# Where three small sums are made in a hybrid encoder layer: pooling additions on VectorE, x split by token groups, norms by a product with ones

## The chip, the cores and the metric

The kernel runs on one core of a Trainium2 chip. The metric is the device time of one execution in microseconds (us). Five engines work side by side, each through its own queue in order: TensorE (PE, with its weight load PEld), VectorE (DVE), ScalarE (ACT), GpSimd (POOL) and SyncE (SP), which issues most DMAs. The median of three runs before the change is 1566.14 us (1560.39 to 1567.87).

## The reference

One layer of a streaming encoder is computed for 1024 prompt tokens and 64 sample tokens, 1088 together, with a model width of 1024, all in fp32:

```python
h = rms_norm(x, norm_mix_g)
q, fl, iv, og, ca, cg, pu = split(h @ w_in)       # 4 x 512, 3 x 256 wide
a_out = hgrn2(q, fl, iv) normed, * silu(og)       # 4 heads, per-token recurrence
b_out = silu(layer_norm(depthwise_conv31(ca * sigmoid(cg))))
c_out = ((window_sum(pu, w) / count - pu) @ pool_w) * pool_scale   # w = 2, 4, 8, 16
x = x + concat(a_out, b_out, c_out) @ w_out
x = x + cross_attention(rms_norm(x, norm_x_g), mem_k, mem_v)       # 256 memory tokens
x = x + square(relu(rms_norm(x, norm_ffn_g) @ w_up)) @ w_down
y = rms_norm(x, final_g)

def rms_norm(x, g):
    return x * rsqrt(mean(x * x, axis=-1) + 1e-6) * g
```

Memory keys and values of the prompt are made from `mem_prompt` by a norm and two projections, and are outputs too, as are the new recurrent state and the last rows of the convolution and the pooling.

## The kernel before, in words

Activations lie transposed: 8 tiles of 128 features by 1088 tokens. Each fp32 operand is split into a high part (`hi`, `wh`) and a low part (`lo`, `wl`), and a product is three matmuls (`mm3`, all recorded under L210). ACT writes the high part, DVE subtracts it to get the low one. A weight block of 128 output features (1024 columns) passes through `prep`: ACT writes `wh`, DVE `wl`, and SP loads the next block. Three split blocks can be held at a time. `dense` multiplies one block with all of x in three groups of 364, 364 and 360 tokens; with `across` the three groups advance together through the 8 input tiles, otherwise group by group. PSUM banks come in two sets of four, `psd` for dense products and `psm` for the rest.

`memory` makes keys, then values (the V loop, 8 blocks, 12 products of 512 columns each). Beside the V loop x is normalised: for each of its 8 tiles DVE multiplies all 1088 tokens by the row `rb` of reciprocal roots, ACT writes `hi` scaled by the gain, DVE writes `lo`. During `memory` and the attention the order on each engine is the order in the program (`inorder`); elsewhere a list scheduler sets it from its own estimate of times.

`mixers` projects h: first the convolution's two pairs (a sigmoid gate `csig` and a product `glu`, for two halves), then per head a gate f and a query q, with the pooling inputs `pu` after head 1. The work of the heads (`head`: 7 levels of a decay tree with PE products and DVE multiplies of `fn` and `q`, then states), of the convolution (`conv`) and of the pooling (`pool`) is fed in pieces between dense products. `pool` makes window sums by doubling: two additions for the half with windows 2 and 4, four for the half with 8 and 16, and one copy each of 64 partitions, all on POOL; then DVE forms the difference to `pu` and PE multiplies it with `poolw`.

A norm of squares summed over tiles in `acc` takes two passes on PE. `rstd_cols` multiplies blocks of 128 tokens of `acc`, as the stationary operand, with one column of ones, so the sums of 128 tokens lie on 128 partitions; ACT takes the root of a few columns, DVE the reciprocal. `bcast_cols` then spreads each column over a row by a product with the identity, and ACT copies the row from PSUM to SBUF. An fp32 product shows as two records. This happens for the attention (1088 tokens), for each half of 544 tokens before the MLP (`rstd_half`, into the tile `masks`), and for three final groups of 416, 416 and 256 tokens.

The MLP (`up`) multiplies by a scheme with 7 products for 8. Its jobs need sums of weight halves (`sw`, `wr`) and split operands (`df`, `th`, `tl`); its outputs are scaled by `masks` on DVE. In the last part each final group adds its tiles to `xr` on DVE, ACT squares them, DVE adds the squares to `facc`, and POOL multiplies `xr` by the row of reciprocal roots before it is stored; the last group is finished by POOL and DVE together.

## Time and profile before

| | |
|---|---|
| median of the runs | 1566.14 us (1560.39 to 1567.87) |
| profiled execution, its time | 1564.72 us |
| profiled execution, its span | 1562.9 us |
| mean granted clock of PE | 0.993 |
| DMA | 150.58 MB, 27.3% of 16 engines' span on the main queue |

The page has the busy time of each engine in the span, and a chain of work followed back from the last instruction. Windows give the same busy times for a stretch, with the granted clock of PE (1.00 is full). In rows of single instructions the first number is the start, the second the length, and the square bracket holds the idle time of the engine before it, with what ended it. In grouped rows the first number behind the bar is the total busy time, the second the mean in ns of one. A length includes some overlap with the next instruction, so the spacing of starts is a little less.

### The profile page before, as it was taken

The numbers are of one execution on the slowest core, as the hardware profiler recorded it, in microseconds if no ns is written. First come the engines' busy times: TensorE is split into PE (matmuls) and PEld (weight loads), VectorE is DVE, ScalarE is ACT, GpSimd is POOL, SyncE is SP. The second block draws the span as 40 slices with busy tenths as digits, with TensorE's granted clock in tenths as the row PEclk, the third lists the DMA queues.
The fourth block names the chain that finished last, engine by engine and source line by source line (L and its number), as shares of the span: only waits on it lengthen the run. The fifth ranks groups of instructions, "written<-read, shape, count | busy, mean of one in ns | idle before, by whom it ended". The sixth has DMA issues, their size and how long they took to land.

```text
span 1562.9 us, 24283 instructions
## 1 busy us (share of the span) xinstructions
PE 1532.2 (98%) x10204; PEld 1486.5 (95%) x10204; DVE 902.6 (58%) x1329; ACT 587.5 (38%) x1072; POOL 123.2 (8%) x101
## 2 busy tenths in 40 slices
PE   8999999999999999999998999999999999999997
PEld 7799898999999999989998999999999999999997
DVE  7638988375654433684579545555585444434434
ACT  7422213556372222463555344444463111111133
POOL 0100001200000000000001222222100000000005
PEclk9999999999999999999999999999999999999999
DMA  9421011010013311223532233232286223211003
GB/s 347 137 83 55 15 41 32 18 41 18 31 66 145 127 55 55 68 78 113 184 113 97 98 112 112 98 112 85 98 320 241 99 100 109 94 59 53 29 1 115
DMA packets 54941, 150.58 MB, mean 96 GB/s; under 512 B 6704, under 2 KB 14384, under 8 KB 54832
## 3 DMA queue, kind: packets, MB, share of 16 engines
q1 hardware_dynamic: 51952, 148.37, 27.3%
q8 instruction: 80, 1.31, 0.3%
q10 hardware_dynamic: 2880, 0.66, 0.2%
q14 instruction: 29, 0.24, 0.0%
HBM read 115.11 MB, written 33.91 MB: 95 GB/s over the span
## 4 chain that ended last, share of the span: by engine, by line
PE 85%; issue 6%; DVE 4%; ACT 2%; POOL 1%; DMA 1%; SPq 0%; POOLq 0%; ACTq 0%; DVEq 0%
PE psd L210 66%; PE psm L210 13%; PE psm L560 3%; POOL xr L137 1%; DVE wl L138 1%; ACT hi L126 1%; PE psm L638 1%; DVE x L138 1%; PE psm L612 0%; PE psm L640 0%; PE psm L542 0%; DMA t<-tt 0%; PE psd L881 0%; DMA wr<-wk 0%; ACT L126 0%
## 5 line engine op out<-in xcount | busy, mean ns | idle before, releaser
L210 PE MATMUL psd<-hi,wl 128*128 128x364 f32 (+3 forms) x1536 | 507.0, 330 | 0.3 <-DVE wl L138 0.3
L210 PE MATMUL psd<-lo,wh 128*128 128x364 f32 (+3 forms) x1536 | 506.2, 330 | 0.9 <-DVE lo L141 0.9
L210 PE MATMUL psd<-hi,wh 128*128 128x364 f32 (+3 forms) x1536 | 505.4, 330 | 1.5 <-ACT hi L126 0.8
L126 ACT ACTIVATE wh<-wr 128x1024 fp32r<-128x1024 f32 (+1 forms) x178 | 160.5, 905 | 483.9 <-PE psd L210 342.8
L210 PEld LDWEIGHTS psd<-hi,wh 128*128 128x128 f32 x1536 | 288.8, 188 | 3.5 <-ACT hi L126 1.5
L210 PEld LDWEIGHTS psd<-lo,wh 128*128 128x128 f32 x1536 | 289.1, 188 | 2.2 <-DVE lo L141 1.5
L210 PEld LDWEIGHTS psd<-hi,wl 128*128 128x128 f32 x1536 | 289.0, 188 | 1.4 <-DVE wl L138 0.6
L138 DVE TENSOR_TENSOR wl<-wr,wh 128x1024 fp32r<-128x1024 f32 (+1 forms) x178 | 185.8, 1049 | 125.3 <-ACT wh L126 125.0
L138 DVE TENSOR_TENSOR xr<-psd,xr 128x364 f32<-128x364 f32 (+3 forms) x192 | 102.0, 533 | 177.4 <-PE psd L210 177.2
L210 PE MATMUL psd<-th,wh 128*128 128x272 f32 x448 | 130.6, 292 | 1.9 <-ACT wh L126 0.8
L210 PE MATMUL psm<-th,wh 128*128 128x272 f32 x448 | 130.4, 292 | 1.9 <-ACT wh L126 1.1
L210 PE MATMUL psd<-th,wl 128*128 128x272 f32 x448 | 129.7, 291 | 2.4 <-DVE wl L138 2.3
L210 PE MATMUL psd<-tl,wh 128*128 128x272 f32 x448 | 129.2, 289 | 0.0
L210 PE MATMUL psm<-th,wl 128*128 128x272 f32 x448 | 129.2, 290 | 0.0
L210 PE MATMUL psm<-tl,wh 128*128 128x272 f32 x448 | 129.1, 289 | 0.0
L210 PEld LDWEIGHTS psm<-th,wh 128*128 128x128 f32 x448 | 84.5, 189 | 3.4 <-ACT wh L126 1.5
L210 PEld LDWEIGHTS psd<-th,wh 128*128 128x128 f32 x448 | 84.6, 189 | 3.1 <-DVE t L138 1.1
L210 PEld LDWEIGHTS psd<-th,wl 128*128 128x128 f32 x448 | 84.4, 189 | 3.2 <-DVE wl L138 3.2
L210 PEld LDWEIGHTS psd<-tl,wh 128*128 128x128 f32 x448 | 84.7, 189 | 0.0
L210 PEld LDWEIGHTS psm<-tl,wh 128*128 128x128 f32 x448 | 84.7, 189 | 0.0
L210 PEld LDWEIGHTS psm<-th,wl 128*128 128x128 f32 x448 | 84.4, 189 | 0.0
L141 DVE SCALAR_TENSOR_TENSOR cacc<-glu,vecs,cacc 128x1118 f32<-128x1118 f32 x60 | 80.6, 1379 | 0.5
(249 smaller groups left out, 2375.0 us busy)
## 6 DMA issues: line engine op xcount, KB each, us to landing
wr<-w_up SPq DMA_DIRECT2D x38, 512.0 KB, 3.9
tt<-t SPq DMA_DIRECT2D x32, 544.0 KB, 3.1
t<-tt SPq DMA_DIRECT2D x32, 544.0 KB, 5.0
wr<-w_down SPq DMA_DIRECT2D x32, 512.0 KB, 3.3
wr<-w_in SPq DMA_DIRECT2D x18, 512.0 KB, 3.2
x<-res SPq DMA_DIRECT2D x16, 544.0 KB, 2.8
wr<-xo SPq DMA_DIRECT2D x16, 512.0 KB, 3.4
x<-xT SPq DMA_DIRECT2D x8, 544.0 KB, 8.3
```

The source lines that it names most:

```text
L126: return self.inorder("act", lambda: self.nc.scalar.activation(out, in_, f, **kw))
L137: return self.inorder("pool", lambda: eng.tensor_tensor(out, a, b, op))
L138: return self.inorder("dve", lambda: self.nc.vector.tensor_tensor(out, a, b, op))
L141: return self.inorder("dve", lambda: self.nc.vector.scalar_tensor_tensor(out, in0, s, in1, op0, op1))
L210: return self.inorder("pe", lambda: self.nc.tensor.matmul(*args, **kw))
L560: mm(pv[:m, c], k[:, c * P:c * P + m], qc[:, :, 1, :], start=True, stop=True)
L638: mm(ps[:w, c * P:c * P + P], sc[:w, s:s + w], vt[:w, s:s + P], start=True, stop=first)
```

## The change

Three edits. The six additions of `pool` move from POOL to DVE; the two copies of 64 partitions stay on POOL. x is normalised and split in 24 pieces, all tiles of the first token group, then of the second, then of the third, with the low part of a piece issued after the multiply of the next one; two pieces go into each round of the V loop from its third on, the other 12 behind it. The first three projections (`csig`, `glu`, `csig`) are multiplied group by group with three weights held, the fourth as before. And `rstd_rows` gets the sums of a segment by one product of a 128x128 matrix of ones with `acc`, which leaves them on all partitions; ACT takes the root of the whole row and DVE its reciprocal. It is used for the attention, both halves before the MLP and the first two final groups; the norms of the memory, of x and of the last group keep the column form.

```diff
+    def rstd_rows(self, sqs, dim, segs=SEGS, rb=None, tag="m"):
+        if rb is None:
+            rb = self.slot(n="rb")
+        for t0, m in segs:
+            ps = self.bank(tag)
+            for i, sq in enumerate(sqs):
+                self.mm(ps[:, :m], self.ones, sq[:, t0:t0 + m], start=i == 0, stop=i == len(sqs) - 1)
+            r = rb[:, t0:t0 + m]
+            self.act(r, ps[:, :m], AF.Sqrt, scale=1.0 / dim, bias=self.eps)
+            self.inorder("dve", lambda: self.nc.vector.reciprocal(r, r))
         return rb
...
             elif k == X_ROWS:
                 rx = self.bcast_rows(r_x, "d")
                 self.act(self.warm, self.eps, AF.Sigmoid)
+                pieces = [(j, g) for g in GROUPS for j in range(KT)]
+                steps = self.normed(hs, pieces, rx)
             if k >= X_ROWS:
-                self.scale_x(k - X_ROWS, rx)
-                hs.append(self.normed(k - X_ROWS))
+                for _ in range(2):
+                    next(steps)
...
-    def normed(self, k):
-        x = self.xraw[k][:, :T]
-        return self.hl(x, self.vec("mix_g", k))
+    def normed(self, hs, pieces, rb):
+        late = None
+        for k, (t0, m) in pieces:
+            if t0 == 0:
+                hs.append((self.slot(F32R, n="hi"), self.slot(F32R, n="lo")))
+            x, (hi, lo) = self.xraw[k][:, t0:t0 + m], (y[:, t0:t0 + m] for y in hs[k])
+            gain = self.vec("mix_g", k)
+            self.tt(x, x, rb[:, t0:t0 + m], MUL)
+            self.act(hi, x, AF.Copy, scale=gain)
+            if late:
+                self.stt(*late)
+            late = (lo, x, gain, hi.bitcast(F32), MUL, SUB)
+            yield
+        self.stt(*late)
...
-            self.dense(self.weights(), xs, ks, plain(sig, AF.Sigmoid), across=first)
+        while len(self.wq) < 3:
+            self.prep()
+        ws, self.wq = self.wq, []
...
+        for g in GROUPS:
+            for w, ev in zip(ws, evs):
+                self.dense(w, xs, ks, ev, groups=[g])
+        for _ in range(2):
+            self.prep()
+        self.dense(self.weights(), xs, ks, evs[3])
...
-        self.tt(s[:, 1:n], pu[:, 1:n], pu[:, 0:n - 1], ADD, gp)
+        self.tt(s[:, 1:n], pu[:, 1:n], pu[:, 0:n - 1], ADD)
...
     def rstd_half(self, c):
-        r = self.rstd_cols([self.accs[c]], CT, D, "m")
-        yield
-        for tts, c0 in ((CT[:4], 0), (CT[4:], 4)):
-            ps = self.bank("m")
-            t0, m = tts[0][0], sum(x[1] for x in tts)
-            self.bcast_cols(ps, r, tts, t0, c0)
-            self.act(self.rb[:, c, t0:t0 + m], ps[:, :m], AF.Copy)
-        yield
+        for seg in ((0, 512), (512, H - 512)):
+            self.rstd_rows([self.accs[c]], D, [seg], self.rb[:, c])
+            yield
...
+            else:
+                acc = self.rstd_rows([acc], D, [(0, m)])
```

How the order moves, at three places. On DVE in the V loop (x are the tiles of x, `wl` the low parts of the next weights), two rounds before:

```order
L138 TENSOR_TENSOR wl_564<-wr_474,wh_563 128x1024
L138 TENSOR_TENSOR x_126<-x_126,rb_541 128x1088
L141 SCALAR_TENSOR_TENSOR lo_583<-x_126,vecs,hi_582 128x1088
L138 TENSOR_TENSOR wl_587<-wr_493,wh_586 128x1024
L138 TENSOR_TENSOR x_148<-x_148,rb_541 128x1088
L141 SCALAR_TENSOR_TENSOR lo_606<-x_148,vecs,hi_605 128x1088
```

and now:

```order
L138 TENSOR_TENSOR wl_568<-wr_474,wh_567 128x1024
L138 TENSOR_TENSOR x_148<-x_148,rb_541 128x364
L141 SCALAR_TENSOR_TENSOR lo_563<-x_126,vecs,hi_562 128x364
L138 TENSOR_TENSOR x_165<-x_165,rb_541 128x364
L141 SCALAR_TENSOR_TENSOR lo_586<-x_148,vecs,hi_585 128x364
L138 TENSOR_TENSOR wl_596<-wr_493,wh_595 128x1024
L138 TENSOR_TENSOR x_203<-x_203,rb_541 128x364
L141 SCALAR_TENSOR_TENSOR lo_591<-x_165,vecs,hi_590 128x364
```

A multiply and its own low part no longer follow each other directly: a low part of the tile before stands between them.

On DVE behind the level chain of head 1 (`st` are the head's states, `ws` and `wu` the window sums), before:

```order
L138 TENSOR_TENSOR q_1757<-q_1757,tot_2018 128x8x64
L616 COPY st_2289<-psm_2290 128x128
L141 SCALAR_TENSOR_TENSOR st_2289<-st_2289,tot_2018,psm_2290 128x128 x2
L141 SCALAR_TENSOR_TENSOR st_2289<-state,tot_2018,psm_2308 128x128
L141 SCALAR_TENSOR_TENSOR st_2289<-st_2289,tot_2018,psm_2290 128x128
```

and now:

```order
L138 TENSOR_TENSOR q_1805<-q_1805,tot_2066 128x8x64
L643 COPY st_2337<-psm_2338 128x128
L138 TENSOR_TENSOR ws_2364<-pu_2013 128x1117
L141 SCALAR_TENSOR_TENSOR st_2337<-st_2337,tot_2066,psm_2338 128x128
L141 SCALAR_TENSOR_TENSOR st_2337<-state,tot_2066,psm_2356 128x128
L141 SCALAR_TENSOR_TENSOR st_2337<-st_2337,tot_2066,psm_2338 128x128
```

The first addition of the pooling, which POOL could start as soon as its input was there, now stands after the whole level chain.

On DVE at the start of the MLP (`tl`, `df` are operands of the second half, `t` the MLP's outputs), before:

```order
L138 TENSOR_TENSOR tl_7197<-res_6634,th_7196 128x544
L247 RECIPROCAL rc_7223<-rc_7223 128x4
L247 RECIPROCAL rc_7223<-rc_7223 32x1
L138 TENSOR_TENSOR df_7250<-res_6563 128x544
L138 TENSOR_TENSOR df_7250<-res_6634 128x544
L138 TENSOR_TENSOR wl_7298<-wr_6864,wh_7297 128x512
```

and now:

```order
L138 TENSOR_TENSOR tl_7215<-res_6664,th_7214 128x544
L138 TENSOR_TENSOR df_7261<-res_6593 128x544
L273 RECIPROCAL masks<-masks 128x512
L138 TENSOR_TENSOR df_7261<-res_6664 128x544
L273 RECIPROCAL masks<-masks 128x32
L138 TENSOR_TENSOR t_7220<-psd_7289,t_7220 128x272
L138 TENSOR_TENSOR wl_7304<-wr_6882,wh_7303 128x512
```

The reciprocal of 4 columns has become one of 512 ahead of an operand's second difference, an output tile and the low part of a weight.

More of the change, by code (lines that the diff above doesn't have):

```diff
@@ L253, in bcast_cols @@
                     start=True, stop=True)
-    def rstd_rows(self, sqs, dim, tag="m"):
-        return self.bcast_rows(self.rstd_cols(sqs, TT, dim, tag), tag)
     def bcast_rows(self, r, tag="m"):
@@ L263, in bcast_rows @@
             self.act(rb[:, t0:t0 + m], ps[:, :m], AF.Copy)
+        return rb
+    def rstd_rows(self, sqs, dim, segs=SEGS, rb=None, tag="m"):
[8 more added lines that the diff above has]
+            self.inorder("dve", lambda: self.nc.vector.reciprocal(r, r))
         return rb
@@ L383, in memory @@
             self.behind.append(lambda m=m, vo=vo: (a["o_memv"][m * P:m * P + P, :], vo[:, :1024]))
-        for j in range(KT - X_ROWS, KT):
-            self.scale_x(j, rx)
-            hs.append(self.normed(j))
+        for _ in steps:
+            pass
         self.expand_masks()
@@ L441, in plain @@
             return ev
-        first = True
-        glus = []
+        while len(self.wq) < 3:
+            self.prep()
+        ws, self.wq = self.wq, []
+        sigs, glus, evs = [], [], []
         for c in range(2):
-            sig = self.slot(n="csig")
-            self.dense(self.weights(), xs, ks, plain(sig, AF.Sigmoid), across=first)
-            first = False
+            sigs.append(self.slot(n="csig"))
             glu = self.slot(n="glu")
@@ L452, in mixers, with ev @@
             nc.scalar.dma_start(glu[:, HIST + TP:2 * HIST + TP], a["cconv"][:, c, :])
-            def ev(b, t0, m):
+            glus.append(glu)
+            def ev(b, t0, m, glu=glu, sig=sigs[c]):
                 e = min(m, TP - t0)
@@ L458, in ev @@
                     self.tt(glu[:, 2 * HIST + t0 + e:2 * HIST + t0 + m], b[:, e:m], sig[:, t0 + e:t0 + m], MUL)
-            self.dense(self.weights(), xs, ks, ev)
+            evs += [plain(sigs[c], AF.Sigmoid), ev]
+        for g in GROUPS:
[4 more added lines that the diff above has]
+        self.dense(self.weights(), xs, ks, evs[3])
+        for c, glu in enumerate(glus):
             nc.scalar.dma_start(a["o_convp"][c * P:c * P + P, :], glu[:, TP:TP + HIST])
             nc.scalar.dma_start(a["o_convs"][c * P:c * P + P, :], glu[:, HIST + T:HIST + T + HIST])
-            glus.append(glu)
         self.bg.append(self.chain(self.conv(glus, mix), 2))
@@ L731, in pool @@
         n = 2 * PH + T
-        gp = nc.gpsimd
         s = self.slot(n="ws")
         u = self.slot(n="wu")
-        self.tt(s[:, 1:n], pu[:, 1:n], pu[:, 0:n - 1], ADD, gp)
+        self.tt(s[:, 1:n], pu[:, 1:n], pu[:, 0:n - 1], ADD)
         yield
         if c == 0:
-            gp.tensor_copy(u[:64, 3:n], s[:64, 3:n])
-            self.tt(u[64:, 3:n], s[64:, 3:n], s[64:, 1:n - 2], ADD, gp)
+            nc.gpsimd.tensor_copy(u[:64, 3:n], s[:64, 3:n])
+            self.tt(u[64:, 3:n], s[64:, 3:n], s[64:, 1:n - 2], ADD)
             res, tmp = u, s
         else:
-            self.tt(u[:, 3:n], s[:, 3:n], s[:, 1:n - 2], ADD, gp)
+            self.tt(u[:, 3:n], s[:, 3:n], s[:, 1:n - 2], ADD)
             yield
-            self.tt(s[:, 7:n], u[:, 7:n], u[:, 3:n - 4], ADD, gp)
+            self.tt(s[:, 7:n], u[:, 7:n], u[:, 3:n - 4], ADD)
             yield
-            gp.tensor_copy(u[:64, PH:n], s[:64, PH:n])
-            self.tt(u[64:, PH:n], s[64:, PH:n], s[64:, 7:n - 8], ADD, gp)
+            nc.gpsimd.tensor_copy(u[:64, PH:n], s[:64, PH:n])
+            self.tt(u[64:, PH:n], s[64:, PH:n], s[64:, 7:n - 8], ADD)
             res, tmp = u, s
@@ L1204, in mlp @@
                     self.act(v, v, AF.Copy, scale=self.vec("final_g", o))
-            tts = [(c, min(P, m - c)) for c in range(0, m, P)]
-            r = self.rstd_cols([acc, sq] if last else [acc], tts, D)
-            ps = self.bank("m")
-            self.bcast_cols(ps, r, tts, 0)
-            self.act(acc[:, :m], ps[:, :m], AF.Copy)
+            if last:
+                tts = [(c, P) for c in range(0, m, P)]
+                r = self.rstd_cols([acc, sq], tts, D)
+                ps = self.bank("m")
+                self.bcast_cols(ps, r, tts, 0)
+                self.act(acc[:, :m], ps[:, :m], AF.Copy)
+            else:
+                acc = self.rstd_rows([acc], D, [(0, m)])
             if not last:
```

3 lines of the change are left out of this document (removed).

## The prediction

> **What bounds the kernel now.** I read the page first: busy times, then the chain that ended last.
>
> ```profile
> PE 1532.2 (98%) x10204; PEld 1486.5 (95%) x10204; DVE 902.6 (58%) x1329; ACT 587.5 (38%) x1072; POOL 123.2 (8%) x101
> PE 85%; issue 6%; DVE 4%; ACT 2%; POOL 1%; DMA 1%; SPq 0%; POOLq 0%; ACTq 0%; DVEq 0%
> ```
>
> TensorE (PE) is busy 1532.2 of 1562.9 us, so only three things can pay: its 31 us of idle time, stretches in which its clock is low, and products that can be left out. The sums by windows show where the first two lie (columns: window, length, busy time of PE, PEld, DVE, ACT, POOL with counts, granted clock, DMA share, GB/s).
>
> ```profile
> 50.00:58.20 8.20, 8.20 (x37) 6.75 (x37) 4.98 (x4) 5.36 (x8) 0.00 (x0) 1.00 0.17 57
> 58.20:69.10 10.90, 8.33 (x26) 5.50 (x25) 8.31 (x7) 5.25 (x6) 0.00 (x0) 0.84 0.29 103
> 61.50:65.00 3.50, 3.50 (x10) 2.69 (x9) 2.23 (x3) 2.15 (x2) 0.00 (x0) 0.51 0.43 150
> 69.10:88.50 19.40, 17.27 (x96) 15.70 (x97) 14.03 (x12) 9.67 (x12) 1.01 (x1) 1.00 0.39 136
> 262.00:278.00 16.00, 13.69 (x76) 13.07 (x76) 10.05 (x11) 1.15 (x4) 6.49 (x3) 0.79 0.11 35
> 269.70:276.60 6.90, 6.45 (x26) 6.30 (x27) 2.35 (x5) 0.00 (x0) 0.00 (x0) 0.51 0.00 0
> 816.00:834.00 18.00, 17.98 (x141) 17.57 (x141) 15.66 (x25) 13.04 (x24) 0.00 (x0) 1.00 0.35 116
> 834.00:861.00 27.00, 22.12 (x156) 20.19 (x156) 27.00 (x37) 14.39 (x26) 5.27 (x3) 0.99 0.25 82
> ```
>
> Three places touch the change. From 58.2 to 88.5 us, where x is normalised and split, PE idles 2.57 + 2.13 = 4.7 us and loses 3.5 x 0.49 = 1.7 us to half clock at 61.5. At 262 to 278 us it idles 2.31 us, and half clock over 6.9 us follows (3.4 us). From 834 to 861 us, at the start of the MLP, VectorE (DVE) is busy 27.00 of 27.00 us and PE idles 4.88 us. The first two are what the change edits; to the third it adds work.
>
> **The x split.** One round of the old V loop, on DVE, ACT and PE:
>
> ```profile
> 59.51 1.22 DVE L138 TENSOR_TENSOR wl<-wr,wh 128x1024 fp32r<-128x1024 f32 x1
> 60.65 1.28 DVE L138 TENSOR_TENSOR x<-x,rb 128x1088 f32<-128x1088 f32 x1
> 63.20 1.35 DVE L141 SCALAR_TENSOR_TENSOR lo<-x,vecs,hi 128x1088 fp32r<-128x1088 f32 x1 [1.27 <-ACT hi L126]
> 64.47 1.22 DVE L138 TENSOR_TENSOR wl<-wr,wh 128x1024 fp32r<-128x1024 f32 x1
> 61.97 1.20 ACT L126 ACTIVATE hi<-x,vecs 128x1088 fp32r<-128x1088 f32 x1 [2.81 <-DVE x L138]
> 63.08 1.04 ACT L126 ACTIVATE wh<-wr 128x1024 fp32r<-128x1024 f32 x1
> 60.78 0.50 PE L210 MATMUL psm<-wl,mhi 128*128 128x512 f32 x1 [1.08 <-DVE wl L138]
> 85.77 0.93 PE L210 MATMUL psd<-hi,wh 128*128 128x364 f32 x4 [0.84 <-ACT hi L126]
> 784.73 0.72 DVE L138 TENSOR_TENSOR acc<-acc,sq 128x544 f32<-128x544 f32 x1
> 87.85 0.84 ACT L126 ACTIVATE csig<-psd 128x364 f32<-128x364 f32 x2 [2.13 <-PE psd L210]
> ```
>
> A round is 64.47 - 59.51 = 4.96 us: wl, x, 1.27 us of waiting for ACT, lo. PE needs 12 products a round, at 8.20 / 37 = 0.222 us each 2.7 us, so DVE sets the pace. A piece of 364 tokens costs DVE, between 0.72 us for 544 and 1.28 for 1088 (1.03 ns per token), 0.535 us, and starts follow each other about 0.08 us closer, so 0.45. ACT takes 0.42. The lo of a piece now stands one piece later, so the 1.27 us wait goes. A new round is wl 1.14, four piece operations 1.8, and a wait of wl: after the second x, ACT does hi (0.42) and wh (0.96), with two handovers of about 0.07, while DVE does one lo (0.45): 1.1 us. Sum 4.0 us. The first round is late for its own reason (ACT loads a table until 52 us) and gains some 0.6; three rounds of 0.95 follow. So the low part of the first w_in weight is ready about 3.5 us sooner, and PE starts the projection that much earlier. From there PE needs the pieces of group 0 only, and group 1 twelve microseconds later: by the order of the changed kernel and 0.45 us per piece they end some 4 us ahead of need. The waits on hi and lo at 82 to 87 us (1.75 us together, the last of them in the row at 85.77) go. Sum **-5.2 us**. Bounds: -6.4 if all the idle time and half clock found above goes (4.7 + 1.7), -2 if a piece costs its full 0.535 us and the new waits draw a half-clock stretch of their own.
>
> **The pooling chain.** POOL, DVE and PE around 265 us:
>
> ```profile
> 262.81 2.07 POOL L137 TENSOR_TENSOR ws<-pu 128x1117 f32<-128x1117 f32 x1 [13.77 <-ACT pu L126]
> 264.94 1.99 POOL L738 COPY wu<-ws 64x1115 f32<-64x1115 f32 x1
> 267.00 2.42 POOL L137 TENSOR_TENSOR wu<-ws 64x1115 f32<-64x1115 f32 x1
> 262.89 3.07 DVE L138 TENSOR_TENSOR wl<-wr,wh 128x1024 fp32r<-128x1024 f32 x1
> 267.44 2.56 DVE L138 TENSOR_TENSOR q<-q,tot 128x544 f32<-128x544 f32 x1
> 280.89 0.71 DVE L138 TENSOR_TENSOR q<-q,tot 128x544 f32<-128x544 f32 x1
> 270.15 1.08 PE L560 MATMUL psm<-q,fn 128*128 128x64 f32 x4 [2.31 <-DVE q L138]
> 293.00:310.00 17.00, 16.95 (x109) 16.04 (x109) 3.69 (x10) 14.04 (x41) 9.75 (x5) 1.00 0.14 37
> ```
>
> The same multiply of q takes 0.71 us alone and 2.56 while POOL adds; wl takes 3.07 instead of 1.22. Each ends when POOL's addition ends. PE waits 2.31 us for that q, and the half clock of 269.7 to 276.6 comes right behind. With no addition on POOL here, q is ready about when PE asks: -2.3 us, and half of the 6.45 us of products that ran at half clock, -3.1: **-5.4 us**. The six additions go to DVE: about 1.3 us each (1.22 for 1024 tokens), 7.8 us. In the changed order the first stands behind the level chain of its head, at about 290 us, and the rest up to about 325. In 293 to 310 us DVE works 3.69 of 17 us, so this cover holds 13 us; without it each addition would cost PE up to 1.3 us. Bounds -5.7 and -2. The two copies stay on POOL.
>
> [...]
>
> **The norms' sums.** The chain of waits shows both old passes for 1088 tokens, and a pass of the wanted kind (a 128x128 fp32 weight on 1088 columns, in the pooling); then reciprocals by size, and the place of the new ones in the attention.
>
> ```profile
> 551.54 2.10 PE psm L210 x18
> 555.16 2.15 PE psm L210 x18
> 312.81 1.89 PE psm L761 x6
> L247 DVE RECIPROCAL rc<-rc 128x8 f32<-128x8 f32 x2 | 0.4, 203 | 2.8 <-ACT rc L126 2.8
> L868 DVE RECIPROCAL mx<-mx 128x2 f32<-128x2 f32 x16 | 2.6, 160 | 1.7 <-ACT pr L126 1.3
> 553.70:563.70 10.00, 10.00 (x65) 9.81 (x66) 0.30 (x2) 1.70 (x5) 0.00 (x0) 1.00 0.01 2
> 563.75 1.51 DVE L141 SCALAR_TENSOR_TENSOR qf<-psd,rb 128x364 f32<-128x364 f32 x3 [9.47 <-PE psd L210]
> 556.09 0.60 ACT L126 ACTIVATE rb<-psm 128x512 f32<-128x512 f32 x1 [2.01 <-PE psm L210]
> 1544.48 9.54 POOL L137 TENSOR_TENSOR xr<-xr,facc 128x416 f32<-128x416 f32 x8 [10.22 <-ACT facc L126]
> 1556.71 2.09 POOL L137 TENSOR_TENSOR y<-xr,facc 128x256 f32<-128x256 f32 x3 [2.69 <-ACT facc L126]
> 1507.63 0.59 DVE L138 TENSOR_TENSOR xr<-psd,xr 128x416 f32<-128x416 f32 x1 [0.46 <-PE psd L210]
> 1509.89 0.59 DVE L138 TENSOR_TENSOR xr<-psd,xr 128x416 f32<-128x416 f32 x1 [0.46 <-PE psd L210]
> ```
>
> PE saves 2.10 + 2.15 - 1.89 = 2.4 us for 1088 tokens, so about 1.25 for each half of 544 and 1.0 for each final group of 416. The price is on DVE. A reciprocal of 2 columns takes 160 ns and of 8 columns 203 ns: 7.2 ns per column over 146 ns. One of 512 columns is then 3.8 us, of 64 0.6, of 32 0.4, of 416 3.1, where a column pass took 0.2. No row is near 512 columns; bounds are 0.7 us for 512 (an addition's 1.03 ns per column) and 7.7 us (twice the slope). I take the slope of the rows.
>
> Attention: the first product ends at about 552.5, the square root takes 0.6, then 2 x 3.8 + 0.6 = 8.2 us of reciprocals run until 561.3. DVE had 0.30 us of work from 553.7 to 563.7, and the first reader (qf) now comes at 563.75 - 2.4 = 561.35. Just hidden; behind it PE has a fourth free bank, 4 us of products. **-2.4**.
>
> First half: PE is full and DVE has gaps; **-1.25**.
>
> Second half: reciprocals of 3.8 + 0.4 - 0.3 = 3.9 us go in at about 817.5 us. DVE has 18 - 15.66 = 2.3 us free until 834 and none until 861, where PE waits for it. What is not absorbed, 1.6 us, lands in PE's waits, and the 1.25 us that PE saves are worth nothing there. Behind the reciprocals wait the low parts of w_up weights and of the operands. I take **+2.0**, between 0 (all absorbed) and +5.6 (nothing absorbed, and another half-clock stretch of 1.7).
>
> [...]
>
> Final groups: two reciprocals of 3.1 us each. PE takes 2.26 us per tile there (1507.63 to 1509.89) and has four banks, so they hide. The last group's y needs POOL, which is busy 9.54 us with the group before. That group starts 1.0 us sooner, but its reciprocal replaces the shorter old path: POOL starts at about 1544.6 again and ends at 1554.1. The y, 2.0 us sooner, wants it at 1554.7. **-2.0**, with 0.6 us to spare; bounds -2.2 and 0.
>
> **Sum.** -5.2 - 5.4 - 2.4 - 1.25 + 2.0 - 2.0 = -14.25 us. The profiled execution, 1564.72 us around a span of 1562.9, becomes 1550.5. It lies 1.4 us under the median of the runs, 1566.14, so I predict **1552 us**.
>
> **Rivals.**
>
> *The gain of the split is given back.* From 140 to 260 us DVE is nearly full with the convolution; if that stretch holds a fixed date, PE only arrives earlier to wait. Against it: the convolution's input comes from PE's own projections and moves with them, and PE has no idle time there now. -9: 1557 us.
>
> *The additions block the heads.* DVE takes 7.8 us more while head 3 starts, and the two copies remain on POOL. If they cost PE what the bound says, -2 instead of -5.4, and a little at the fs and q tiles: 1556 us. Against it stands the row of 293 to 310 us.
>
> *The start of the MLP costs its upper bound*, +5.6 instead of +2.0: 1555.6; with the POOL margin at the end missed as well, 1558.
>
> *Everything goes*: every term at its better bound, split -6.4, pool -5.7, final -2.2, and the MLP absorbs the reciprocals. -18 us: 1548 us.
>
> *Row-wide reciprocals set the pace* (the slower side). This one mechanism decides from about 18 ns per column. At 20 ns, 1088 columns take 22 us, against 8.2 us of cover and 4 us of bank: +9.9 in the attention. 544 columns put 8.7 us more than forecast on the full DVE of the MLP, clock included. In the last groups 416 columns take 8.3 us, and POOL and the y come 5 us late. -14.2 + 23.6 = +9.4: 1575.5 us. For it: 512 columns are far from 8. Against it: three column counts lie on one line of 7 ns.
>
> **How the numbers follow.** Forecast 0.52 (1549 to 1555), everything goes 0.14, split given back 0.12, additions block 0.10, MLP's upper bound 0.07, reciprocals set the pace 0.05. A change under 0.5%, 7.8 us, can't be told from none: faster is below 1558.3, slower above 1574. The first four cases (0.88) are faster but for their edges, 0.10 together, and so is 0.03 of the MLP case, whose rest is within 0.5% with those edges. Faster 0.81, same 0.14, slower 0.05. The range 1545 to 1560 takes in all cases but the slow one and the outer edges.
>
> **What would show it.** x and lo of 128x364 at about 0.45 us spacing and a round of about 4 us; PE without waits on hi or lo after 70 us. No DVE tensor_tensor over 1.5 us from 250 to 275 us, and clock 1.00 there. Reciprocals of 128x512 at about 3.8 us; ones products of some 0.9 us for 512 columns. DVE full from 817 to the end of that stretch, and PE idle there 6 to 7 us instead of 4.88. The forecast is wrong if reciprocals cost double, if PE waits anew in 290 to 330 us, or if the round stays near 5 us.

## The result, and the profile after

The changed kernel took 1552.3 us in the median (1550.4 to 1552.4), the kernel before beside it 1565.4; the ratio is 0.9916, with a 95% interval of 0.9902 to 0.9931. In a second series it was 1552.3 against 1562.4, ratio 0.9934 (0.9917 to 0.9951). It is faster, at the predicted time. The gain is another matter. The sum of the prediction was -14.25 us. Between the two profiled executions it was 12.4 us (spans 1562.9 and 1550.6), and in the second series, with 29 executions of the kernel before, 10.

The page of the changed kernel, busy times and the chain that ended last:

```profile
PE 1520.3 (98%) x10114; PEld 1474.5 (95%) x10114; DVE 927.4 (60%) x1366; ACT 587.9 (38%) x1076; POOL 108.5 (7%) x95
PE 93%; DVE 3%; ACT 2%; issue 1%; POOL 1%; DMA 0%; SPq 0%; POOLq 0%; ACTq 0%; DVEq 0%
```

TensorE has 90 product records and 12 us less, VectorE 25 us more. The sums by windows of the changed kernel (columns as in the prediction: window, length, busy time of PE, PEld, DVE, ACT, POOL, granted clock, DMA share, GB/s):

```profile
...
58.20:65.90 7.70, 6.15 (x24) 4.20 (x24) 5.49 (x11) 4.30 (x6) 0.00 (x0) 1.00 0.41 136
65.90:88.50 22.60, 21.94 (x130) 21.64 (x131) 20.34 (x38) 14.52 (x25) 1.01 (x1) 1.00 0.39 119
262.00:278.00 16.00, 16.00 (x127) 15.10 (x126) 6.76 (x12) 3.44 (x9) 0.00 (x0) 1.00 0.01 2
540.40:555.00 14.60, 14.60 (x83) 13.61 (x83) 12.17 (x9) 3.64 (x5) 0.00 (x0) 1.00 0.13 48
694.80:701.70 6.90, 6.90 (x25) 5.84 (x25) 2.02 (x5) 1.84 (x5) 0.00 (x0) 0.51 0.00 0
803.00:823.00 20.00, 18.65 (x137) 17.46 (x138) 19.78 (x27) 14.15 (x25) 0.00 (x0) 1.00 0.32 109
823.00:850.00 27.00, 21.61 (x149) 19.67 (x149) 27.00 (x36) 14.01 (x24) 5.30 (x3) 0.97 0.24 81
```

From 58.2 to 88.5 us TensorE idles 1.55 + 0.66 = 2.2 us instead of 4.7, at full clock. From 262 to 278 us it idles no longer. In the attention's norm (540.4 to 555) VectorE works 12.17 of 14.60 us and TensorE does not notice. Two rows are worse: 6.9 us at half clock at 694.8, where the kernel before had full clock, and TensorE now idles 1.35 us from 803 to 823, before the MLP.

VectorE in the changed kernel: a round of the V loop, the multiply of q at the place of the former collision, and the new reciprocals (last fence: groups by line and form, with the mean in ns).

```profile
57.36 1.23 DVE L138 TENSOR_TENSOR wl<-wr,wh 128x1024 fp32r<-128x1024 f32 x1 [1.11 <-ACT wh L126]
58.50 0.53 DVE L138 TENSOR_TENSOR x<-x,rb 128x364 f32<-128x364 f32 x1
58.95 0.59 DVE L141 SCALAR_TENSOR_TENSOR lo<-x,vecs,hi 128x364 fp32r<-128x364 f32 x1
59.45 0.53 DVE L138 TENSOR_TENSOR x<-x,rb 128x364 f32<-128x364 f32 x1
...
61.60 1.23 DVE L138 TENSOR_TENSOR wl<-wr,wh 128x1024 fp32r<-128x1024 f32 x1 [1.11 <-ACT wh L126]
...
265.29 0.71 DVE L138 TENSOR_TENSOR q<-q,tot 128x544 f32<-128x544 f32 x1
```

```profile
L273 DVE RECIPROCAL rb<-rb 128x512 f32<-128x512 f32 x2 | 6.6, 3324 | 0.7 <-ACT rb L126 0.7
L273 DVE RECIPROCAL rb<-rb 128x416 f32<-128x416 f32 x2 | 5.5, 2748 | 1.4 <-ACT rb L126 1.4
...
L273 DVE RECIPROCAL masks<-masks 128x32 f32<-128x32 f32 x2 | 0.7, 344 | 0.0
```

A round is 61.60 - 57.36 = 4.24 us (predicted 4.0, before 4.96). q takes 0.71 us. A reciprocal of 512 columns takes 3.32 us (predicted 3.8), and from 32 to 512 columns it costs 2980 / 480 = 6.2 ns per column (predicted 7.2).

### The profile page after: what moved, and what is told of

The parts are those of the page before. It is cut to its first block, busy times and chain, and to the rows that moved or that the text cites. A ratio compares the mean times of both kernels' runs of the same rounds, so it can differ in the third digit from the quotient of the medians.

```text
span 1550.6 us, 24142 instructions
## 1 busy us (share of the span) xinstructions
PE 1520.3 (98%) x10114; PEld 1474.5 (95%) x10114; DVE 927.4 (60%) x1366; ACT 587.9 (38%) x1076; POOL 108.5 (7%) x95
## 4 chain that ended last, share of the span: by engine, by line
PE 93%; DVE 3%; ACT 2%; issue 1%; POOL 1%; DMA 0%; SPq 0%; POOLq 0%; ACTq 0%; DVEq 0%
PE psd L210 73%; PE psm L210 13%; PE psm L587 3%; DVE wl L138 1%; ACT wh L126 1%; POOL xr L137 1%; PE psm L665 1%; PE psd L907 1%; PE psm L639 0%; PE psm L667 0%; DMA wr<-wk 0%; PE psm L569 0%; PE psm L677 0%; DVE tl L138 0%; DVE sw L138 0%
```

## The experiments

**A common measure.** Between fixed marks of the program the stages turned out to repeat to 0.1 us from profile to profile, but for one thing: stretches at half clock. So each kernel is shown by what its one profiled execution spent from mark to mark, and "+n" behind a time counts the beats at half clock (3.41 us each) in that stage. Marks are first products on TensorE: of the V loop, of the values, of the states of head 0 and of head 1 (`psm<-ident,fn`), of the attention's sum, of the scores, of the two halves' sums, the last of the MLP's up part, and the first of the final groups' sums; the last stage ends with TensorE's last product. Between the marks that are left out nothing differs by more than 0.3 us; ahead of the first one the profiles differ by up to 1.4 us.

| stage, us | before | pool | split | rows | changed | changed again |
|---|---|---|---|---|---|---|
| V loop to values | 108.44 +2 | 106.86 +1 | 102.13 | 106.76 | 102.13 | 102.15 |
| head 0 to head 1 | 53.16 +2 | 47.74 | 53.28 +2 | 51.76 +1 | 47.70 | 47.69 |
| attention's sum to scores | 96.73 | 96.73 | 96.73 | 94.24 | 94.24 | 94.24 |
| scores to first half's sum | 119.60 | 120.56 +1 | 119.66 | 120.57 +1 | 122.10 +2 | 122.17 +2 |
| first to second half's sum | 47.53 | 47.52 | 47.52 | 46.07 | 46.07 | 46.08 |
| second half's sum to up's end | 350.82 +1 | 348.49 | 349.27 | 351.47 +1 | 351.80 +1 | 351.44 +1 |
| final groups | 35.40 | 35.38 | 35.38 | 34.84 | 34.53 | 34.77 |
| median, us | 1562.4 | 1558.8 | 1559.9 | 1559.6 | 1552.3 | 1552.3 |

**Pooling additions alone** (the kernel before with `gp` taken out of the additions of `pool`):

```diff
-        self.tt(s[:, 1:n], pu[:, 1:n], pu[:, 0:n - 1], ADD, gp)
+        self.tt(s[:, 1:n], pu[:, 1:n], pu[:, 0:n - 1], ADD)
...
```

> The kernel before with only the pooling chain's six additions moved to VectorE. Theory (each part acts by itself): TensorE's wait of 2.31 us for q at 270 us goes, and so does the half-clock stretch of 6.9 us behind it; -5.4 us, about 1560 us beside a median of 1565.4, and no multiply of q or wl above 1.5 us between 250 and 280 us. Rival 1 (the additions block the heads): new waits of TensorE between 290 and 330 us, and about -2 us. Rival 2 (half-clock stretches fall where the program's own beat puts them, whether or not there is a wait of 2.3 us): the wait of 2.3 us goes, but a stretch of 6.9 us comes back somewhere else, and the gain is 2.3 us or less.

Measured: ratio 0.9974 (0.9962 to 0.9986), which is -4.1 us (-5.9 to -2.2). By windows:

```profile
264.00:275.00 11.00, 11.00 (x77) 10.79 (x78) 5.93 (x12) 0.95 (x2) 0.00 (x0) 1.00 0.14 48
290.00:310.00 20.00, 20.00 (x120) 17.82 (x119) 10.20 (x18) 17.91 (x43) 0.00 (x0) 1.00 0.12 37
```

TensorE is full at both places, so the rival that blocks the heads falls. The stage from head 0 to head 1 is 5.4 us shorter than in the profile of before, as predicted. One half-clock beat now stands at 702.4 us, where the profile of before had none. That is rival 2 in part, which had two such beats and a gain of at most 2.3 us; of that more below.

**The x split alone** (`normed` by pieces and the grouped projections, with the old `pool`, norms and final groups):

```diff
+                pieces = [(j, g) for g in GROUPS for j in range(KT)]
+                steps = self.normed(hs, pieces, rx)
...
+        for g in GROUPS:
+            for w, ev in zip(ws, evs):
+                self.dense(w, xs, ks, ev, groups=[g])
```

> The kernel before with only the split of x by token groups, its shifted low parts, and the first projections by groups. Theory: the first values product starts some 5 to 6 us sooner (144.49 us before) and everything behind keeps it: 1559 to 1560 us. The collision at 262 to 278 us stays as it was (a q of about 2.5 us, TensorE waits 2.3 us). Rival (the gain is given back in the convolution's stretch from 140 to 260 us): TensorE gets new waits there, and the time is above 1563 us.

Measured: 0.9985 (0.9971 to 1.0000), or -2.3 us (-4.5 to 0). Everything behind the values keeps the gain: the next stage lasts 89.8 us in all profiles, so the rival of a gain given back falls. The collision is unchanged (TensorE, timeline):

```profile
264.04 1.30 PE L577 MATMUL psm<-q,fn 128*128 128x64 f32 x5 [2.31 <-DVE q L138]
```

**The norms' sums alone** (`rstd_rows`, `rstd_half` and the final groups of the change, the rest as before):

```diff
+            self.act(r, ps[:, :m], AF.Sqrt, scale=1.0 / dim, bias=self.eps)
+            self.inorder("dve", lambda: self.nc.vector.reciprocal(r, r))
...
```

> The kernel before with only the norms' sums by a product with ones and row-wide reciprocals. Theory: -2.4 us at the attention, -1.3 at the first half of the scores, +1 at the start of the MLP, -0.9 in the final groups: -3.5 us, about 1562. Rival (the sum by the prediction's own terms, MLP +2.0 and final groups -2.0): -3.7 us in all but with the MLP's start 2 us later and the last group 2 us sooner. Rival (the 6.9 us stretch at half clock that the changed kernel shows at 694.8 us comes from the new norms): the same stretch appears here some 11 us later, near 706 us, behind waits of 0.5 us, and the gain is only 1 us. If it does not appear here, the stretch hangs on where the waits fall, and not on the new norms.

Measured: 0.9983 (0.9970 to 0.9997), or -2.7 us (-4.7 to -0.5). By stages: -2.5 at the attention, -1.45 at the first half, and -0.55 in the final groups instead of -2.0. The half-clock beat near 704 us is there, but so it is in the kernel with the pooling alone, which has none of the new norms. So it does not come from them.

The sum of the three, -9.1 us, is about what the whole change gives in that series, -10.3 (-13.0 to -7.7): the parts act one by one.

**The changed kernel again** (no edit):

> The changed kernel once more, with a profile. Theory (half-clock stretches hang on the beat of the program, which is the same in every execution): the stretch from 694.8 to 701.7 us is there again at the same place, and the time is 1550 to 1552.5 us. Rival (they fall by chance, execution by execution): the stretch is missing or elsewhere, and the span is up to 3.4 us shorter for one stretch less.

Measured: 1551.0 to 1554.0 us. Half clock from 694.6 us again, for 6.8 us. The other one is at 827.7 us, where the first profile had 848.4, so the places do not simply repeat from execution to execution; what decides is worked out below.

**Pooling additions left on GpSimd, but later.** A tiny copy makes GpSimd's first addition wait until head 1's state is there:

```diff
+        if c == 0:
...
+            first = gp.tensor_copy(e0, self.mark[:, 0:1])
...
+        if c == 0:
+            with self.after(first):
+                self.tt(s[:, 1:n], pu[:, 1:n], pu[:, 0:n - 1], ADD, gp)
```

> The kernel before with the additions of the pooling chain still on GpSimd, but the first one made to start only behind the level chain of its head, so that it no longer meets the multiply of q. Theory (what cost time was the meeting of the two engines just there, not GpSimd's speed): q takes 0.7 us again, TensorE's wait of 2.3 us at about 268 us goes, no half clock stretch there, and the next heads start 5 us sooner than before, as with the additions on VectorE; 1558 to 1560 us. VectorE's operations of 293 to 310 us stretch to 2 or 3 us instead, without a wait of TensorE. Rival (GpSimd's additions do harm wherever they stand): new waits of TensorE between 290 and 330 us, and no gain.

Measured: 0.9983 (0.9969 to 0.9996); head 0 to head 1 takes 47.69 us, as with the additions on VectorE, and TensorE waits nowhere from 250 to 335 us. GpSimd, then VectorE:

```profile
285.85 1.11 POOL L750 COPY wu<-ws 64x1115 f32<-64x1115 f32 x1
...
291.30 2.05 POOL L138 TENSOR_TENSOR ws<-pu 128x1117 f32<-128x1117 f32 x1 [1.35 <-issue]
```

```profile
286.08 1.96 DVE L139 TENSOR_TENSOR wl<-wr,wh 128x1024 fp32r<-128x1024 f32 x1 [0.24 <-ACT wh L127]
291.34 2.10 DVE L142 SCALAR_TENSOR_TENSOR ws<-wu,vecs,pu 128x64 f32<-128x64 f32 x1
```

So it was the meeting, not the engine. A copy on GpSimd stretches an operation of VectorE as well: wl, 1.21 us at 261.62 us in this run, takes 1.96 and ends 1.08 us after GpSimd's copy does (286.96 us). And 64 columns, 0.29 us at 315.43 us, take 2.10 us, to the end of GpSimd's addition. Nobody on TensorE waits for those two.

**The shift of the low parts alone** (whole tiles, the low part of a tile issued behind the next tile's multiply) **and the token groups alone** (pieces, each low part right behind its high part; this second diff is against the x split):

```diff
         self.tt(x, x, rb[:, :T], MUL)
+        self.act(hi, x, AF.Copy, scale=gain)
+        if self.late:
+            self.stt(*self.late)
+        self.late = (lo, x, gain, hi.bitcast(F32), MUL, SUB)
```

```diff
-            if late:
-                self.stt(*late)
-            late = (lo, x, gain, hi.bitcast(F32), MUL, SUB)
+            self.stt(lo, x, gain, hi.bitcast(F32), MUL, SUB)
```

> The kernel before with whole tiles of x as before, in one group, but the low part of each tile issued one tile later, so that the wait of 1.27 us for ScalarE's high part is filled. Theory (the shift of the low parts gives the gain up to the first projection, the token groups the rest): the round goes from 4.96 to about 4.5 us, the first projection starts about 1.5 to 2 us sooner, and the waits on low parts at 82 to 87 us stay, or grow; values start 1 to 2 us sooner than in an undisturbed kernel before (142.9), where the full split had 138.4. Rival (the shift is all of it): 138.4 to 139.5. Rival (the groups are all of it): 142.5 to 143.5 and a round that stays at 5.

> The kernel with the x split alone, but without the shift: the low part of each token group's piece follows at once behind its high part, so that VectorE waits for ScalarE in every piece. Theory (shift and groups each give a part): the round is 4.8 to 5.0 us, where the whole split has 4.24; the first projection starts at about 67.5 us, as with undivided tiles, but the waits on high and low parts at 82 to 87 us go, and the first values product starts at 140.5 to 141.5 us, between 142.9 of whole tiles and 138.4 of the full split. Rival (the groups are all of it): 138.4 to 139. Rival (the groups alone give nothing): 142.5 or later.

Measured: shift 0.9995 (0.9983 to 1.0007), groups 0.9999 (0.9990 to 1.0008). VectorE with the shift alone, then with the groups alone:

```profile
60.14 1.23 DVE L138 TENSOR_TENSOR wl<-wr,wh 128x1024 fp32r<-128x1024 f32 x1 [0.96 <-ACT wh L126]
...
64.78 1.23 DVE L138 TENSOR_TENSOR wl<-wr,wh 128x1024 fp32r<-128x1024 f32 x1 [0.96 <-ACT wh L126]
```

```profile
58.54 0.60 DVE L141 SCALAR_TENSOR_TENSOR lo<-x,vecs,hi 128x364 fp32r<-128x364 f32 x1 [0.67 <-ACT hi L126]
59.49 1.23 DVE L138 TENSOR_TENSOR wl<-wr,wh 128x1024 fp32r<-128x1024 f32 x1 [0.35 <-ACT wh L126]
...
64.49 1.23 DVE L138 TENSOR_TENSOR wl<-wr,wh 128x1024 fp32r<-128x1024 f32 x1 [0.35 <-ACT wh L126]
```

The shift alone brings the round to 4.64 us, and V loop to values takes 105.9 us instead of 106.8, with one beat at half clock at 45.8 us. In the profile with the final norm in columns such a beat at 45.2 us made this stage of the full split 103.7 us instead of 102.1, so without it the shift alone would take some 104.3. The groups alone leave the round at 5.00 us (0.67 us of waiting in each piece, 0.35 at the weight); V loop to values takes 107.4 us, with two beats at half clock behind the waits of that loop, and the values start at 144.2 us, not at 140.5 to 141.5. How much of that is half clock (at most 3.4 us) stays open; the times show no gain, which is what the rival "nothing" said. Together the two give 102.13. With short pieces the handover of 0.67 us comes twice in a round, and the shift hides it.

**Two of the row-wide norms put back to columns**, together and one by one:

```diff
     def rstd_half(self, c):
-        for seg in ((0, 512), (512, H - 512)):
-            self.rstd_rows([self.accs[c]], D, [seg], self.rb[:, c])
-            yield
+        if c == 0:
+            for seg in ((0, 512), (512, H - 512)):
+                self.rstd_rows([self.accs[c]], D, [seg], self.rb[:, c])
+                yield
+            return
+        r = self.rstd_cols([self.accs[c]], CT, D, "m")
...
-            if last:
...
+            if t0 == 0:
+                acc = self.rstd_rows([acc], D, [(0, m)])
+            else:
```

> The changed kernel with two of its five row-wide norms put back to columns: the second half's before the MLP and the second final group's. Theory (both cost more than they save where they stand): TensorE's new waits of 1.28 us at 811 us and of 1.6 us at 1538.5 us go, the MLP starts 1 us sooner and the last group ends 0.6 us sooner, and the half-clock stretch behind the waits of 820 to 850 us comes less often: 1550 us, 1.5 to 3 us below the changed kernel. Rival (TensorE's longer column path costs what the waits did): within 0.5 us of the changed kernel, 1552.3.

> The changed kernel with the second half's norm before the MLP in columns again. Theory (what is lost at the start of the MLP hangs on these reciprocals): the waits of 1.28 us at 811 us and of 1.35 us at 824 us go, the MLP's first part ends 1 to 2.5 us sooner (1154.65 us in the changed kernel), and the time is 1550.5 to 1551.5 us. Rival (the column path costs TensorE what the waits did): no change.

> The changed kernel with the norm of the second final group in columns again, the first one in rows. Theory (the reciprocal of 416 columns makes the evictions of the last group late): the wait of 1.6 us at 1538.5 us goes, TensorE needs 1.0 us more for the sums, and the last group ends 0.6 us sooner; 1551.7 us. Rival (GpSimd's multiplies, not the reciprocal, hold the evictions up): the wait stays, and the end is 1 us later.

| stage, us | changed | half in columns | final in columns | both |
|---|---|---|---|---|
| second half's sum to up's end | 351.80 +1 | 350.77 +1 | 351.42 +1 | 349.28 |
| final groups | 34.53 | 34.21 | 33.81 | 33.81 |
| median, us | 1552.3 | 1549.9 | 1551.6 | 1550.2 |
| ratio to before | 0.9934 | 0.9920 | 0.9930 | 0.9920 |

Interval of the ratios: 0.9906 to 0.9935, 0.9914 to 0.9946, and 0.9903 to 0.9936. By windows, the kernel with the half in columns:

```profile
803.00:823.00 20.00, 19.55 (x152) 18.91 (x151) 17.68 (x29) 14.47 (x26) 0.00 (x0) 1.00 0.31 105
```

TensorE idles 0.45 us there instead of 1.35, and VectorE works 17.68 us instead of 19.78. The wait of 1.28 us is gone, the one of 1.35 us shrinks to 0.82. The last group, in the changed kernel (VectorE, TensorE), and then with the second final group in columns (VectorE):

```profile
1529.65 2.75 DVE L273 RECIPROCAL rb<-rb 128x416 f32<-128x416 f32 x1 [1.37 <-ACT rb L126]
...
1533.25 1.83 DVE L138 TENSOR_TENSOR facc<-facc,fsq 128x256 f32<-128x256 f32 x2
...
1535.34 2.21 DVE L138 TENSOR_TENSOR facc<-facc,fsq 128x256 f32<-128x256 f32 x2
```

```profile
1540.15 0.38 PE L210 MATMUL psm<-ones,facc 128*128 128x1 f32 x2 [1.60 <-DVE facc L138]
```

```profile
1533.71 1.35 DVE L138 TENSOR_TENSOR facc<-facc,fsq 128x256 f32<-128x256 f32 x1 [0.48 <-ACT fsq L126]
...
1535.88 0.43 DVE L138 TENSOR_TENSOR facc<-facc,fsq 128x256 f32<-128x256 f32 x1 [0.48 <-ACT fsq L126]
```

The reciprocal of 416 columns holds the evictions up, and then two pairs of additions of `facc` meet GpSimd's multiplies (0.42 us becomes 0.9 to 1.1 in the mean); the sum waits 1.60 us for the last. In columns only one addition is stretched. The 0.7 us between 34.53 and 33.81 is not that wait alone, though: the two runs with waits put in elsewhere (below) keep the row-wide norm and the wait of 1.60 us, and their final groups take 33.78 and 33.77 us. In them half clock begins only behind TensorE's last product, in the changed kernel 2.6 us ahead of the end of that product. The kernel with both in columns has no half clock in either stage, and is the best in them. Its six executions were 1549.75 to 1550.75 us, against 1551.0 to 1554.0 for the changed kernel in the series of its repetition; the first series of the changed kernel reached down to 1550.4, and the intervals of the ratios overlap. About 2 us better, likely, not proved by the times.

**Waits put in on purpose.** In each profile the half-clock stretches start on one grid of 3.41 us: in the kernel before, 61.5 - 44.5 is 5 beats of it, 269.7 - 61.5 is 61, and 860.2 - 269.7 is 173. What decides which beat is hit? In the down projection, where TensorE has no wait for 350 us, chains of 1 to 5 short waits were put in:

```diff
+    def turns(self, n):
+        x = self.ident[:, :8]
+        for i in range(n + 1):
+            ps = self.bank("m")
+            self.mm(ps[:, :8], self.ident, x, start=True, stop=True)
+            if i < n:
+                x = self.small(8, "turn")
+                self.act(x, ps[:, :8], AF.Copy)
...
+                if o % 2:
+                    self.turns((4 * i + o // 2) % 5 + 1)
```

> The changed kernel with waits put in on purpose where TensorE is otherwise full (1165 to 1509 us): behind every second tile of the down projection a chain of 1, 2, 3, 4 or 5 turns in which a product of 8 columns waits for ScalarE's copy of the product before it, some 0.5 to 0.6 us of idle time each, 0.5 to 2.8 us in all, 28 places. The six profiles so far have half-clock stretches in multiples of 3.41 us that start on one grid of 3.41 us, and put in order by TensorE's idle time within a beat of that grid, the beats with 1.5 us or more are followed by half clock in 9 of 10 cases, those between 0.98 and 1.47 us in none of 10. Theory (idle time in one beat decides, over single waits together): no stretch behind 1 or 2 turns, one behind nearly all places of 4 and 5 turns, and about half of those of 3, whichever way the beat cuts them. Rival 1 (one unbroken wait of about 2 us is needed): no stretch at all, since no single wait is above 0.7 us. Rival 2 (the stretches fall by chance): as many behind 1 and 2 turns as behind 4 and 5.

That run told nothing: the small products slid in between others, and TensorE waited 0.4 us in all 370 us (1580.9 us, for the products themselves). So they were held in their place:

> As the run with waits put in on purpose, but with the small products held in their place behind the tile's last product and ahead of the next tile's first (in that run they slid in between other products, and TensorE waited 0.4 us in all). 28 chains of 1, 2, 3, 4 or 5 turns of some 0.5 us of idle time each. Theory (idle time summed over one beat of the 3.41 us grid decides, from about 1.5 us): no half-clock stretch behind 1 or 2 turns, about half of those of 3, nearly all of 4 and 5. Rival 1 (one unbroken wait of about 2 us is needed): none. Rival 2 (by chance): no relation with the number of turns.

Measured: 1654.7 us. A chain of 4 turns (TensorE), and pairs of a beat with such waits and what follows it (by windows: 2, 4 and 5 turns):

```profile
1449.70 0.39 PE L210 MATMUL psm<-turn,ident 128*128 128x8 f32 x2 [0.93 <-ACT turn L126]
1450.36 0.39 PE L210 MATMUL psm<-turn,ident 128*128 128x8 f32 x2 [0.27 <-ACT turn L126]
...
1451.67 0.39 PE L210 MATMUL psm<-turn,ident 128*128 128x8 f32 x2 [0.27 <-ACT turn L126]
```

```profile
1418.02:1421.43 3.41, 2.22 (x16) 2.04 (x14) 1.55 (x3) 1.30 (x3) 0.00 (x0) 1.00 0.00 0
1421.43:1424.84 3.41, 3.41 (x21) 3.41 (x22) 1.01 (x2) 0.00 (x0) 0.00 (x0) 1.00 0.48 154
1448.77:1452.17 3.40, 1.67 (x11) 1.39 (x11) 1.68 (x2) 1.41 (x5) 0.00 (x0) 1.00 0.10 18
1452.17:1455.58 3.41, 3.41 (x13) 3.41 (x13) 0.00 (x0) 0.00 (x0) 0.00 (x0) 0.50 0.34 136
1544.33:1547.74 3.41, 1.68 (x11) 1.31 (x10) 1.82 (x3) 1.65 (x5) 0.00 (x0) 1.00 0.00 0
1547.74:1554.57 6.83, 6.56 (x23) 6.47 (x24) 0.54 (x1) 0.18 (x1) 0.00 (x0) 0.50 0.00 0
```

| turns | idle time of the chain, us | chains | followed by half clock |
|---|---|---|---|
| 1 | 0.7 to 0.9 | 6 | 0 |
| 2 | 1.2 to 1.3 | 6 | 1 |
| 3 | 1.5 to 2.0, in one chain 0 | 6 | 2 |
| 4 | 1.7 to 2.2 | 5 | 5 |
| 5 | 2.0 to 2.5 | 5 | 5 |

Of the beats at full clock, every one with 1.198 us or more of idle time (13) is followed by a beat at half clock, and none with 1.191 us or less (22 with over 0.25 us). Single waits are 0.3 to 0.9 us. So it is the sum over one beat that counts, and with 2 or 3 turns where the beat cuts the chain: rival 1 (one long wait) and rival 2 (chance) fall. The edge in idle time, with 7 ns between the two sides, should not be taken as a threshold: the small products between the waits, 0.39 us for 8 columns, count as busy here (more on that under "What no step had"). Four chains of 5 turns run 0.27 us into the half-clock beat, and there a second one follows.

## Why the prediction was right, and where it was not

Means over the profiled executions with and without each part; the two with waits put in are left out. "Without" are, in the first row, before, pool, rows and the deferred additions (the shift and the groups by themselves are in neither); in the second, the five with the collision; in the third, the six with columns at the attention; in the fourth, all that have not the x split, the pooling and the row-wide norms together; in the sixth, those with columns there; in the last, those with columns in both final groups (one group in each form is in neither).

| step of the prediction | predicted | this pair of profiles | mean over the profiles |
|---|---|---|---|
| x split | -5.2 | -6.3 | 102.4 - 107.2 = -4.8 |
| pooling chain | -5.4 | -5.5 | 47.7 - 52.0 = -4.3 |
| attention's norm | -2.4 | -2.5 | 94.2 - 97.2 = -3.0 |
| (scores to first half) | 0 | +2.5 | 121.8 - 120.3 = +1.5 |
| first half | -1.25 | -1.45 | -1.45 |
| second half, MLP | +2.0 | +1.0 | 351.5 - 349.3 = +2.2 |
| final groups | -2.0 | -0.9 | 34.6 - 35.4 = -0.8 |
| sum | -14.25 | -13.1 | -10.7 |

The pair's sum is 0.7 us more than the 12.4 us of the spans, since the V loop began 0.6 us later in the profile after, and the stages left out took 0.1 us more. The last column's sum is close to what the series measured (10).

**x split.** The round came out at 4.24 instead of 4.0 us: x takes 0.45 us from start to start, but lo 0.50 (58.95 to 59.45), and each weight waits 1.11 us as foreseen. No wait on hi or lo is left behind 67 us. Of the pair's 6.3 us some 1.6 is half clock: the old loop took 108.44 us with two beats, and 106.8 in three other profiles. By the mean, -4.8, the term of -5.2 was nearly right, and inside its bounds.

**Pooling chain.** Mechanism right: q, wait and half clock are gone together, and the later start on GpSimd shows that the meeting was the cause. The two stretched operations do not end with GpSimd's addition, as the prediction reads its rows, but 1.08 us (wl, 265.96 for 264.88) and 0.58 us (q, 270.00 for 269.42) behind it, about their usual length (1.22 and 0.71 us), as if each had run only when it was done. The size of the half clock was taken as a fixed property of the place. The same wait of 2.31 us cost two beats, one or none (TensorE and windows, norms alone, then groups alone):

```profile
268.65 1.52 PE L570 MATMUL psm<-q,fn 128*128 128x64 f32 x12 [2.31 <-DVE q L138]
```

```profile
270.46:273.87 3.41, 3.41 (x14) 3.28 (x14) 2.05 (x4) 0.00 (x0) 0.00 (x0) 0.51 0.00 0
```

```profile
269.30:272.70 3.40, 2.82 (x22) 2.75 (x23) 1.25 (x4) 0.00 (x0) 0.00 (x0) 1.00 0.00 0
```

Head 0 to head 1 takes 53.2 us with two beats, 51.8 with one, 50.2 with none, and 47.7 without the wait. So the wait is worth 2.5 us and its half clock 0 to 3.0, 1.8 in the mean. The prediction took 3.1, what its one profile showed. This is the term that was mis-sized.

**Attention and first half.** -2.5 and -1.45, for -2.4 and -1.25. The reciprocals hide, as the row of 540.4 to 555 shows. The mean of -3.0 has a half-clock beat in it that no step had: near 548 us, behind the old sums by columns, two of the six profiles with columns there have one (98.29 us instead of 96.73), and none of the eight with rows.

**Second half.** The reciprocals landed where foreseen, on the full VectorE before the MLP; TensorE's idle time there is 1.35 + 5.39 = 6.7 us. All six profiles with the row-wide norm at this place (the two with waits put in among them) have a half-clock beat there, between 827 and 852 us, and two of the eight without it do. By the measure worked out below, a beat that begins 19.6 to 21.0 us behind the second half's sum falls under the edge in all six, and in none of the eight. So the new waits bring the half clock more often. By the mean +2.2, so the +2.0 holds, though in the pair it was +1.0, since the profile before had such a beat too.

**Final groups.** "PE takes 2.26 us per tile there (1507.63 to 1509.89) and has four banks, so they hide" failed. The banks cover the reciprocal itself, but behind it the additions of `facc` fall into GpSimd's multiplies, and the last sum has no bank to hide behind. With that wait alone the stage gains 1.6 us (33.78 in the runs with waits put in, for 35.40); the rest of what is missing is half clock, which begins 1.9 to 3.3 us ahead of the end of TensorE's last product in four of the six profiles with rows in both groups, and at most 0.2 us ahead of it in the other ten. GpSimd, named as the margin of 0.6 us, was not the limit: it is free 2.31 us before y. In the changed kernel:

```profile
1532.48 9.55 POOL L137 TENSOR_TENSOR xr<-xr,rb 128x416 f32<-128x416 f32 x8 [8.85 <-DVE rb L273]
1544.34 2.09 POOL L137 TENSOR_TENSOR y<-xr,facc 128x256 f32<-128x256 f32 x3 [2.31 <-ACT facc L126]
```

**What no step had.** Half clock from 694.8 us, +1.5 us by the mean. Before it TensorE has the same two waits in both kernels, 0.47 and 0.50 us, and then products of 64 columns, and the kernel before had full clock behind them in its profile. Twelve of the fourteen profiles show one or two half-clock beats at this place, though no beat there has more than 1.0 us of idle time. The beat ahead of it in the changed kernel and its counterpart in the kernel before, then some of the 64-column products (kernel before):

```profile
691.40:694.80 3.40, 2.43 (x21) 2.21 (x19) 2.12 (x8) 1.13 (x5) 0.00 (x0) 1.00 0.07 22
703.20:706.60 3.40, 2.42 (x14) 1.63 (x12) 3.25 (x10) 2.33 (x8) 0.00 (x0) 1.00 0.60 234
```

```profile
706.55 0.30 PE L210 MATMUL psd<-pl,kvh 128*128 128x64 f32 x1
706.68 0.28 PE L210 MATMUL psd<-ph,kvl 128*128 128x64 f32 x1
706.80 0.28 PE L210 MATMUL psd<-ph,kvh 128*128 128x64 f32 x1
```

TensorE is equally busy in both beats, yet only the first was followed by half clock. The columns that it streams tell the two apart. In the kernel before, products of 272 columns follow each other every 0.127 us and those of 512 every 0.227, so a column takes 0.417 ns; in an undivided fp32 product twice that (512 columns: 0.43 us). The 64 columns above are thus 0.03 us of streaming in a record of 0.28. Summed up by this estimate, each product's streaming set 0.16 us ahead of its record's end (0.13 to 0.18 give the same), the first beat has 0.47 us of streaming and the second 1.47. In the fourteen profiles, from 20 us to 25 us before the end, all 45 full-clock beats with 1.27 us of streaming or less were followed by half clock, and of the other 6125, all with 1.34 or more, one (1.44, at this place in the kernel with the later additions). The beats of 1.198 and 1.191 us of idle time above have 1.13 and 1.40. Behind 12 of the 58 half-clock beats a second one follows, and the same number of columns separates these from the rest: in the kernel before it is 0.72 us of columns, counted at full clock, in the beat at 269.7 us, which a second one follows, and 1.7 in those at 44.5, 61.5 and 860.2, which none follows. The beats near 44 and 548 us fit in too: no wait is ahead of them, but the norms' sums by columns, products of a single column (kernel before: 18 records from 41.52 us take 2.04 us, and the beat ahead of 44.46 has 1.16 us of streaming). The edge was found in these profiles; no run was made to test it.

At 694.8 us it is a draw, then: in all fourteen profiles, a beat that begins 0.1 to 0.8 us ahead of the wait of 0.47 us is followed by two half-clock beats, one that begins 0.3 to 1.0 us behind its start by one, and with a beat 1.7 to 1.9 us ahead of it there is none, whatever the kernel. With the whole change it is two in most, without it one or none; whether the change makes that cut likelier is not shown.

**The time.** The predicted 1552 us leant on a median of three executions, 1566.1 us, and on a profile with 11.7 us of lost clock. Four later series of the kernel before had medians of 1562.1 to 1563.1; 29 of its executions ran from 1558.6 us at a granted clock of 0.996 to 1567.7 at 0.990, and 0.006 x 1557 = 9.3 us is that whole spread. Some 3 of the 11.7 us lie behind TensorE's last product, where they cost nothing. The base was 3.5 us too high (1566.1 for 1562.5) and the gain 4 us too large (14.25 for 10), and the two cancelled: that the time came out to 0.3 us was luck, while most of the terms held.

## What to carry to other kernels

Read a stall and the half clock behind it as two terms: the first is fixed (2.5 us for the wait for q), the second (0 to 3.0 us there) is drawn by where a beat of 3.41 us cuts a stretch in which TensorE streams few columns, and one profile shows one draw; count it at its mean, and compare stages between marks over several profiles instead of whole times. When one engine's work stretches another's operations (q took 0.71 us alone and 2.56 beside GpSimd's addition), moving the one in time can be worth as much as moving it to another engine (head 0 to head 1 took 47.7 us either way here). A wide reciprocal (3.32 us for 512 columns) was free only where its engine had slack until the next thing that TensorE needed: the same form saved 2.5 us in the attention, and cost 2.2 before the MLP.

## What the runs showed of the hardware

In the fourteen profiles TensorE's granted clock fell to half for a beat of 3.41 us behind every full-clock beat in which it streamed columns for 1.27 us or less (45 of 45), whether the rest was waits or products of few columns, and behind 1 of 6125 with 1.34 us or more (an estimate from columns, worked out above). Idle time is a rougher sign. In the run with waits put in, all 13 beats with 1.198 us of it or more were followed by half clock, summed over waits of 0.3 to 0.9 us; elsewhere, between 45 and 900 us, 15 of 18 beats with 1.5 us or more were, and 2 of 29 with 1.0 to 1.5 us. Near 44 and 548 us half clock came with no wait at all. Within a profile the stretches start on one grid (5, 61 and 173 beats apart in the kernel before), and from profile to profile the grid cuts the same place differently: the wait of 2.31 us cost two beats, one or none.
